# One of three projections of a hybrid decoder step goes from plain products to Strassen's scheme, and a merge pair becomes the last unit of the recurrent stage

## The chip, the cores and the metric

The kernel runs on one core of one Trainium2 chip. The metric is device time in microseconds (us) of one execution; lower is better. The engines are named as the profile names them: PE (matmuls; PEld is its loading of weights), DVE (vector engine), ACT (scalar engine), POOL (GpSimd) and SP, from whose queue nearly all transfers are issued.

## What is computed

One step of a decoder layer for a prompt of 2048 rows and for 8 single-row samples, all in float32, with D = 1024. Cut to what matters here:

```python
h = rmsnorm(x, norm_g) * (1 + scale) + shift
q, k, v, ga, xr, gr, ma, mr = split(h @ w_in)
ya = band_attention(rmsnorm(q), rmsnorm(k), v) * silu(ga)
yr = rglru(causal_conv(xr)) * silu(gr)
merged = sigmoid(ma) * (ya @ w_pa) + sigmoid(mr) * (yr @ w_pr)
y = x + gate * (merged @ w_out)
```

## The kernel before

**Precision and slots.** Every float32 operand of a large product is split into a high and a low part in a shorter format (`split_to`: ACT casts the high part, DVE subtracts it to get the low part). A product is then three matmuls per 128 rows of the contraction: high by high, high by low, low by high. The unit of planning is a slot: 4 row blocks by 3 matmuls = 12 matmuls of 128 x 512 into one PSUM bank.

**Two halves.** The prompt is worked on in two halves of 1024 rows (s = 0, then s = 1; the samples ride along in the second). Each half runs attention and then a line of slots (`stages`), transposed: channels on partitions, positions along the free dimension, 512 at a time. The line of a half is: three units that finish the previous stage, the attention's gate, four pairs for the recurrent branch (`rnn(p)`), pairs for the merge gates (`merge`), then the projection of the attention's branch (`pa`), that of the recurrent branch (`pr`) and the output (`out`).

**Two kinds of unit.** `Plain` makes 128 output channels by 1024 positions in 4 slots: per unit 2 splits of weights, and 2 evacuations of a PSUM bank. `Fast` is Strassen's scheme (in Winograd's form) on a 2 x 2 grid: 256 output channels by 1024 positions in 7 slots, where plain products take 8. It works on sums and differences of the four blocks of weights (`s1` to `s4`, on DVE) and of the activations (T1 to T4); per unit 7 splits of weights, 3 banks that are copied out by ACT, 3 that DVE adds to them, and one that is used from PSUM. `pair(a, b)` alternates the slots of two units. Before the change `w_in`'s columns and the output use `Fast`; `pa` and `pr` use `Plain`.

**What sets the order.** `Line` keeps, for each slot, a list of other work with a rank (evacuations first, then splits of weights, then forms of activations, then the chains of the recurrent branch, then stores and loads). All engines run in their program's order, so this list is the order. A unit's weights are loaded 7 slots ahead of their use and split 2 slots ahead. An unsplit input is loaded 3 slots ahead of its split (`load_split`).

**Around the change.** The recurrent chain of one pair (`chain`, 4 pieces of 512 positions: convolution, split, gates, a scan) begins 12 slots after the pair's first slot and ends some 24 slots after the pair's last one. The order of pairs before is: attention gates 2 and 3; rnn 0; merge 1; rnn 1; merge 2; rnn 2; merge 3; rnn 3; then `pa`. The activations of the input `h` (7 forms by 4 blocks) fill all 28 large tiles of the ring S until the last unit, marked `final`, gives them back. The ring B has 35 tiles of 512 columns for everything else. Tensors in DRAM: `yad` (attention times gate, the input of `pa`), `tmad` and `tmd` (tanh of the merge gates), `t1d` (what `pa` leaves), `sgd`, `yrd`, `mgd`. `phase_h`, in the first half alone, prepares the second half's `h` (loads of `x`, row norms, transposes) beside `pa`.

```python
EVAC, SIDE, SPLIT, FORM, CHAIN, LATE, STORE, LOAD = range(8)
PROD = (("A11", "x11", "X"), ("A12", "x21", "Y"), ("S2", "T2", "X"), ("S1", "T1", "Y"), ("S3", "T3", "X"),
        ("S4", "x22", "Y"), ("A22", "T4", "X"))
AHEAD, LOADS = 2, 7
```

Of the kernel before, what the change touches and what calls it, by code (L numbers as in the profile page):

```python
# [12 lines left out]
F32 = mybir.dt.float32  # L13
# [28 lines left out]
def tile_hybrid_step(ctx: ExitStack, tc: tile.TileContext, x_prompt, x_sample, cache_k, cache_v, state_conv,  # L42
# [191 lines left out]
    V.memset(q1, 0.25)  # L234

# [107 lines left out]
    for t in wgr + [hsF, yaF]:  # L343
# [8 lines left out]
                                     for t in ("yad", "tmad", "tmd", "sgd", "yrd", "t1d", "mgd"))  # L352
    Gd = dp.tile([P, D], F32, tag="Gd", name="Gd")
# [57 lines left out]
    def phase_h(line, t0):  # L411

        def group(g, t0):
            xts = []

            def load(i):
                xts.append(S([D]))
                r0 = 1024 + g * 512 + i * P
                ld.dma_start(xts[i], xp[r0:r0 + P, :])

            def turn(f):
                ps = PT()
                for i in range(4):
                    T_.transpose(ps[:, i * P:(i + 1) * P], xts[i][:, f * P:(f + 1) * P], ident)
                line.after(1, EVAC, lambda: h_evac(1, ps, 512, f, g * 512, None))
                if f == KT - 1:
                    free(*xts)

            for i in range(4):
                line.on(t0 + 2 * i, LOAD, lambda i=i: load(i))  # L430
                line.on(t0 + 4 + 2 * i, CHAIN, lambda i=i: rms_rows([xts[i][:, h * 512:(h + 1) * 512] for h in range(2)], P))
# [669 lines left out]
    class Fast:  # L1101
# [3 lines left out]
        def __init__(self, line, F, src, evac, samples=None, base=None, late=False):  # L1105
            self.line, self.F, self.src, self.evac, self.samples = line, F, src, evac, samples
            self.base, self.late, self.early = base, late, 0
# [27 lines left out]
        def place(self, s):  # L1135
# [6 lines left out]
            for i, j in ((0, 0), (1, 0), (0, 1), (1, 1)) if late else ((0, 0), (1, 0), (1, 1), (0, 1)):  # L1142
                line.on(s[0] - (3 if late and j == 1 else LOADS + self.early), LOAD, lambda i=i, j=j: self.load(i, j))
# [109 lines left out]
    def stages(s, hT, hT1=None, side=None):  # L1253
# [348 lines left out]
        pair(attn_gate(2), attn_gate(3))  # L1602
        for p in range(4):
            end = rnn(p)
            if p < 3:
                pair(merge(OFF_MA, p + 1, tmad, maS), merge(OFF_MR, p + 1, tmd, mrS))
# [23 lines left out]
        yax, yrx = xtiles(), xtiles()  # L1630
        quarters = [(4 * h + k, c) for h in range(2) for c in range(2) for k in range(4)]
        for i, (k, c) in enumerate(quarters):
            load_split(yad, yax, k, c, rnn_end - 11 + 10 * i // 16, 3)

        def load_pair_rows(w, c0):
            wr = w[:, c0:c0 + P].rearrange("(G gg j d) c -> G gg d j c", G=2, gg=2, j=4)

            def load(t, h):
                for gg in range(2):
                    ld.dma_start(t[gg * 64:gg * 64 + 64], wr[h, gg])  # L1640
            return load

        def pa(f):
            tm = {}

            def load(c):
                tm[c] = Tt([512])
                ld.dma_start(tm[c], chunk(tmad, f, c))

            def evac(c, ps):  # L1650
                V.scalar_tensor_tensor(tm[c], tm[c], 1.0, ps, op0=ALU.add, op1=ALU.mult)
                line.after(1, STORE, lambda: store(c))
# [525 lines left out]
```

## Time and profile before

| | before |
|---|---|
| median of 3 runs | 1969.95 us (1969.76 to 1970.19) |
| the profiled execution, its own time | 1970.57 us |
| its span, first to last instruction | 1968.9 us |
| PE busy | 1918.9 us (97%), 11504 matmuls |
| DVE busy | 1376.8 us (70%) |
| ACT busy | 985.0 us (50%) |
| POOL busy | 391.3 us (20%) |
| DMA | 286.61 MB, mean 146 GB/s |

The profiled execution's own time is 1.7 us over its span and 0.6 us over the median. Busy shares are means over the whole execution; a stage is read from a window of its own. Matmuls overlap in the records, so the price of one is read from the starts of two groups and the count between them, not from the mean duration.

### The profile page before, as it was taken

How to read it: one execution, taken by the hardware profiler on the slowest of the kernel's cores; microseconds unless marked ns; L12 is line 12 of the kernel's file. 1: busy time of each engine (PE TensorE's matmuls, PEld its weight loads, DVE VectorE, ACT ScalarE, POOL GpSimd, SP SyncE). 2: the span in 40 equal slices, each digit the busy share in tenths (PEclk: the TensorE clock that was granted, in tenths of full speed). 3: DMA queues.
4: the chain of work that ended last, by engine and by line, in shares of the span. 5: the costliest groups of instructions: out<-in, count | busy, mean ns of one | idle time of the engine just before them, and what ended most of it. 6: DMA issues, size and time to landing. Idle time of an engine off the chain costs nothing. (4 is left out here: it accounts for less than half of the span.)

```text
span 1968.9 us, 32371 instructions
## 1 busy us (share of the span) xinstructions
PE 1918.9 (97%) x11504; PEld 1569.0 (80%) x11504; DVE 1376.8 (70%) x2862; ACT 985.0 (50%) x2167; POOL 391.3 (20%) x476
## 2 busy tenths in 40 slices
PE   6899999999999999999999999999999999999999
PEld 4798986778888878877898888777887887777777
DVE  3557778567887876587735776776677879755965
ACT  4435665336575766323424555543475667532321
POOL 2213443000111113150022333300010201111600
PEclk9899999999999999999999999999999999999999
DMA  9521125652433567976611111544233325458673
GB/s 280 175 65 51 48 77 158 202 171 93 138 118 100 176 190 251 330 243 191 228 47 49 55 34 51 160 124 151 82 119 108 126 93 167 144 170 300 214 236 108
DMA packets 307686, 286.61 MB, mean 146 GB/s; under 512 B 57073, under 2 KB 224229, under 8 KB 307486
## 3 DMA queue, kind: packets, MB, share of 16 engines
q1 hardware_dynamic: 307398, 282.41, 45.8%
q0 software_dynamic: 128, 2.15, 0.3%
q8 instruction: 90, 1.47, 0.3%
q14 instruction: 70, 0.57, 0.1%
HBM read 200.69 MB, written 85.93 MB: 146 GB/s over the span
## 5 line engine op out<-in xcount | busy, mean ns | idle before, releaser
L60 PE MATMUL pg<-S,B 128*128 128x512 f32 (+1 forms) x4224 | 1003.7, 392 | 4.2 <-DVE B L60 3.8
L60 PEld LDWEIGHTS pg<-S,B 128*128 128x128 f32 (+1 forms) x4224 | 773.9, 188 | 188.6 <-issue 11.1
L60 DVE TENSOR_TENSOR B<-B,B 128x512 fp32r<-128x512 f32 (+1 forms) x732 | 540.9, 761 | 145.8 <-ACT B L60 136.0
L60 PE MATMUL pq<-S,B 128*128 128x512 f32 (+2 forms) x1920 | 412.2, 379 | 6.7 <-DVE B L60 6.6
L60 PEld LDWEIGHTS pq<-S,B 128*128 128x128 f32 (+1 forms) x1920 | 317.0, 188 | 85.2 <-DVE B L60 10.6
L60 POOL TENSOR_TENSOR B<-B,B 128x512 f32<-128x512 f32 x128 | 191.4, 1513 | 921.5 <-DVE B L60 363.5
L60 ACT CAST B<-B 128x512 fp32r<-128x512 f32 x468 | 279.9, 617 | 111.4 <-DVE B L60 71.5
L60 PE MATMUL pg<-B,S 128*128 128x256 f32 x1872 | 243.3, 286 | 0.0
L60 PEld LDWEIGHTS pg<-B,S 128*128 128x128 f32 x1872 | 228.1, 189 | 10.1 <-issue 9.4
L60 DVE TENSOR_TENSOR S<-B,S 128x512 fp32r<-128x512 f32 x184 | 144.6, 814 | 25.9 <-ACT S L60 25.7
L60 ACT CAST S<-B 128x512 fp32r<-128x512 f32 x184 | 109.3, 620 | 94.0 <-DVE B L60 40.7
L60 ACT ACTIVATE B<-B 128x512 f32<-128x512 f32 (+1 forms) x150 | 93.1, 629 | 117.0 <-DVE B L60 109.0
L60 ACT ACTIVATE B<-B,M 128x129 f32<-128x129 f32 x260 | 102.6, 396 | 91.3 <-DVE M L60 87.1
L60 DVE SCALAR_TENSOR_TENSOR B<-B,pg 128x512 f32<-128x512 f32 x78 | 53.1, 682 | 72.9 <-PE pg L60 63.1
L60 ACT COPY H<-pt 128x256 f32<-128x256 f32 (+1 forms) x55 | 18.5, 337 | 160.9 <-PE pt L60 160.9
L60 DVE TENSOR_TENSOR B<-pq,B 128x512 f32<-128x512 f32 x96 | 65.9, 686 | 44.3 <-PE pq L60 38.3
L60 POOL TENSOR_TENSOR B<-B,M 128x512 f32<-128x512 f32 x64 | 68.6, 1093 | 122.8 <-DVE M L60 122.8
L60 ACT COPY B<-pg 128x512 f32<-128x512 f32 x80 | 46.8, 586 | 89.4 <-PE pg L60 81.1
L60 ACT ACTIVATE B<-pg 128x512 f32<-128x512 f32 x76 | 45.2, 595 | 85.3 <-PE pg L60 85.3
L60 POOL TENSOR_TENSOR M<-M,mhalf 128x8 f32<-128x8 f32 (+4 forms) x70 | 83.8, 1198 | 5.8
L60 DVE SCALAR_TENSOR_TENSOR B<-B,VT,B 128x512 f32<-128x512 f32 x96 | 81.2, 846 | 2.3
L60 DVE TENSOR_TENSOR B<-pt,mcT 128x512 f32<-128x512 f32 x64 | 41.7, 686 | 47.4 <-ACT B L60 45.5
(201 smaller groups left out, 1718.6 us busy)
## 6 DMA issues: line engine op xcount, KB each, us to landing
B<-in_w_in_dram SPq DMA_DIRECT2D x144, 256.0 KB
B<-in_w_in_dram SPq DMA_DIRECT2D x128, 128.0 KB
B<-yad SPq DMA_DIRECT2D x56, 256.0 KB
B<-hd SPq DMA_DIRECT2D x48, 256.0 KB
B<-in_w_out_dram SPq DMA_DIRECT2D x48, 256.0 KB
S<-in_w_ada_dram SPq DMA_DIRECT2D x32, 256.0 KB
S<-in_x_prompt_dram SPq DMA_DIRECT2D x16, 512.0 KB
hd<-B SPq DMA_DIRECT2D x32, 256.0 KB
```

The lines of the kernel that those rows point to most:

```text
L60: ins = fn(*args, **kw)
```

## The change

The projection `pa` is made of 4 `Fast` units in 2 pairs (28 slots) where 8 `Plain` units (32 slots) stood, in each half. Its evacuation goes to DVE for one block in four; for the other three ACT adds 1 to the merge gate's tanh (`plus`) and POOL multiplies. The four differences of its input are made earlier, by `differences`: 4 times 4 loads from `yad`, 4 subtractions on POOL, 4 stores to the new DRAM tensor `yfd`. The 7 forms by 4 blocks are then loaded and split by `form_y` (28 loads and splits where 16 stood). The pair of attention gates 2 and 3 moves behind rnn 0, and each merge pair moves one place, so that merge 3 is the last pair before `pa`. `phase_h` starts 8 slots later, counted from the recurrent stage's end, and holds its rows in tiles of ring B. Weights of `pa` are loaded 5 slots ahead.

```diff
+    onec = C([P, 1], tag="onec")
+    V.memset(onec, 1.0)
...
+    yfd = dp.tile([2, 4, 4, P, 512], F32, tag="yfd", name="yfd")
...
-                xts.append(S([D]))
+                xts.append([Tt([512]) for _ in range(2)])
                 r0 = 1024 + g * 512 + i * P
-                ld.dma_start(xts[i], xp[r0:r0 + P, :])
+                for h in range(2):
+                    ld.dma_start(xts[i][h], xp[r0:r0 + P, h * 512:(h + 1) * 512])
...
-            self.base, self.late, self.early = base, late, 0
+            self.base, self.late, self.early, self.ahead = base, late, 0, LOADS
...
-                line.on(s[0] - (3 if late and j == 1 else LOADS + self.early), LOAD, lambda i=i, j=j: self.load(i, j))
+                line.on(s[0] - (3 if late and j == 1 else self.ahead + self.early), LOAD, lambda i=i, j=j: self.load(i, j))
...
-        pair(attn_gate(2), attn_gate(3))
         for p in range(4):
             end = rnn(p)
-            if p < 3:
-                pair(merge(OFF_MA, p + 1, tmad, maS), merge(OFF_MR, p + 1, tmd, mrS))
+            if p == 0:
+                pair(attn_gate(2), attn_gate(3))
+                ga_end = len(seq)
+            else:
+                pair(merge(OFF_MA, p, tmad, maS), merge(OFF_MR, p, tmd, mrS))
         seq[-1][0].final = True
         rnn_end = len(seq)
 
...
-        for i, (k, c) in enumerate(quarters):
-            load_split(yad, yax, k, c, rnn_end - 11 + 10 * i // 16, 3)
...
+
+        FY = {n: [None] * 4 for _, n, _ in PROD}
+
+        def differences(k, t):
+            x = {}
+
+            def load():
+                for n, f, c in (("x11", k, 0), ("x12", k, 1), ("x22", k + 4, 1), ("x21", k + 4, 0)):
+                    x[n] = Tt([512])
+                    ld.dma_start(x[n], chunk(yad, f, c))
+
+            def sub(a, b, o, n):
+                G_.tensor_tensor(x[o], x[a], x[b], op=ALU.subtract)
+                line.after(2, STORE, lambda: st.dma_start(yfd[s, n, k], x[o]))
+
+            def first():
+                sub("x12", "x11", "x11", 0)
+                sub("x22", "x12", "x12", 2)
+
+            def second():
+                x["T2"] = Tt([512])
+                sub("x22", "x11", "T2", 1)
+                sub("x21", "T2", "x21", 3)
+
+            line.on(t, LOAD, load)
+            line.on(t + 4, FORM, first)
+            line.on(t + 6, FORM, second)
+            line.on(t + 9, EVAC, lambda: free(*x.values()))
+
+        for k in range(4):
+            differences(k, ga_end + (6, 11, 27, 32)[k])
+
+        def form_y(n, k, t):
+            src = {"x11": (k, 0), "x21": (k + 4, 0), "x22": (k + 4, 1)}.get(n)
+            box = []
+
+            def load():
+                box.append(Tt([512]))
+                ld.dma_start(box[0], chunk(yad, *src) if src else yfd[s, int(n[1]) - 1, k])
+
+            def split():
+                FY[n][k] = S([2, 512], F32R)
+                split_to(FY[n][k][:, 0, :], FY[n][k][:, 1, :], box[0])
+                free(box[0])
+
+            line.on(t - 3, LOAD, load)
+            line.on(t, FORM, split)
+
+        for i, (n, k) in enumerate([(n, k) for _, n, _ in PROD for k in range(4)]):
+            form_y(n, k, rnn_end - 9 + 18 * i // 25)
+
+        def pa(p):
+            tm = {}
+
+            def load_w(t, i, j):
+                wr = w_proj_attn[0][:, (2 * p + i) * P:(2 * p + i + 1) * P].rearrange(
+                    "(G gg j d) c -> G gg d j c", G=2, gg=2, j=4)
                 for gg in range(2):
-                    ld.dma_start(t[gg * 64:gg * 64 + 64], wr[h, gg])
-            return load
-
-        def pa(f):
-            tm = {}
-
-            def load(c):
-                tm[c] = Tt([512])
-                ld.dma_start(tm[c], chunk(tmad, f, c))
-
-            def evac(c, ps):
-                V.scalar_tensor_tensor(tm[c], tm[c], 1.0, ps, op0=ALU.add, op1=ALU.mult)
-                line.after(1, STORE, lambda: store(c))
-
-            def store(c):
-                st.dma_start(chunk(t1d, f, c), tm[c])
-                free(tm[c])
-
-            z, d = zS[:, f:f + 1, :], maS[:, f:f + 1, :]
-            u = Plain(line, yax, load_pair_rows(w_proj_attn[0], f * P), evac,
-                      sample(yaF, z, lambda: V.scalar_tensor_tensor(d, d, 1.0, z, op0=ALU.add, op1=ALU.mult)))
-            t0 = len(seq)
-            seq.extend((u, n) for n in range(4))
-            for c in range(2):
-                line.on(t0 + c, LOAD, lambda c=c: load(c))
-            return u
-
-        for f in range(KT):
-            u = pa(f)
-        u.gone = set(u.order)
+                    ld.dma_start(t[gg * 64:gg * 64 + 64], wr[j, gg])
+
+            def load(i, j):
+                tm[i, j] = Tt([512])
+                ld.dma_start(tm[i, j], chunk(tmad, 2 * p + i, j))
+
+            def plus(i, j):
+                A.activation(tm[i, j], tm[i, j], AF.Identity, bias=onec)
+
+            def evac(i, j, x, t):
+                y = tm[i, j]
+                if t is None:
+                    V.scalar_tensor_tensor(y, y, 1.0, x, op0=ALU.add, op1=ALU.mult)
+                else:
+                    G_.tensor_tensor(y, y, x, op=ALU.mult)
+                    free(t)
+                line.after(1 if t is None else 2, STORE, lambda: store(i, j))
+
+            def store(i, j):
+                st.dma_start(chunk(t1d, 2 * p + i, j), tm[i, j])
+                free(tm[i, j])
+
+            z, d = zS[:, 2 * p:2 * p + 2, :], maS[:, 2 * p:2 * p + 2, :]
+            u = Fast(line, FY, load_w, evac,
+                     sample(yaF, z, lambda: V.scalar_tensor_tensor(d, d, 1.0, z, op0=ALU.add, op1=ALU.mult)))
+
+            def loads(t0):
+                for n, i, j in ((1, 0, 0), (4, 1, 1), (5, 0, 1), (6, 1, 0)):
+                    line.on(t0 + 2 * n - 4, LOAD, lambda i=i, j=j: load(i, j))
+                    if n < 6:
+                        line.on(t0 + 2 * n, LATE, lambda i=i, j=j: plus(i, j))
+
+            return u, loads
+
+        for p in range(0, 4, 2):
+            (a, la), (b, lb) = pa(p), pa(p + 1)
+            a.ahead = b.ahead = 5
+            t0 = pair(a, b)
+            la(t0)
+            lb(t0 + 1)
+        b.final = True
         pa_end = len(seq)
         for i, (k, c) in enumerate(quarters):
-            load_split(yrd, yrx, k, c, pa_end - 8 + i // 2 if i < 8 else pa_end - 3 + (i - 8) // 2, 3)
+            load_split(yrd, yrx, k, c, pa_end - 10 + 3 * i // 4, 3)
 
         def pr(f):
             ts = {}
...
+            phase_h(line, rnn_end + 12)
             for k in range(KT):
...
-            line.steps(sample_attn(), range(7, 30), SIDE)
+            line.steps(sample_attn(), list(range(7, 27)) + [38], SIDE)
```

Three places in the engines' order. On DVE where the projection starts: below, before the change, are the 11 rows from the last recurrent pair's two last slots into the projection's first units. B is ring B, S ring S (an S row is a split of an activation), pg and pq are PSUM, VT holds the convolution's weights.

```order
L60 TENSOR_TENSOR B_7819<-B_7691,B_7818 128x512
L60 SCALAR_TENSOR_TENSOR B_7816<-B_7816,pg_7419 128x512
L60 SCALAR_TENSOR_TENSOR B_7847<-B_7548,VT_105,B_7847 128x512 x3
L60 TENSOR_TENSOR B_7874<-B_7743,B_7873 128x512
L60 TENSOR_TENSOR B_7882<-B_7847,B_7881 128x512
L60 SCALAR_TENSOR_TENSOR B_7824<-B_7824,pg_7803 128x512
L60 SCALAR_TENSOR_TENSOR B_7879<-B_7879,B_7767 128x512
L60 SCALAR_TENSOR_TENSOR B_7856<-B_7856,pg_7826 128x512
L60 TENSOR_TENSOR B_7929<-B_7800,B_7928 128x512
L60 SCALAR_TENSOR_TENSOR B_7877<-B_7932,B_7877 128x512
L60 TENSOR_TENSOR B_7976<-B_7858,B_7975 128x512
```

The same place after the change, 12 rows of the projection's first two slots:

```order
L60 TENSOR_TENSOR B_7829<-B_7826,B_7829 128x512
L60 TENSOR_TENSOR B_7826<-B_7974,B_7826 128x512
L60 TENSOR_TENSOR B_8020<-B_7835,B_8019 128x512
L60 TENSOR_TENSOR B_8023<-B_7869,B_7872 128x512
L60 TENSOR_TENSOR S_8025<-B_7916,S_8025 128x512
L60 TENSOR_TENSOR B_7869<-B_7866,B_7869 128x512
L60 TENSOR_TENSOR B_7866<-B_8023,B_7866 128x512
L60 TENSOR_TENSOR B_8054<-B_7875,B_8053 128x512
L60 TENSOR_TENSOR S_8057<-B_7954,S_8057 128x512
L60 TENSOR_TENSOR S_8060<-B_7956,S_8060 128x512
L60 SCALAR_TENSOR_TENSOR B_7944<-B_8028,B_7944 128x512
L60 TENSOR_TENSOR B_8087<-B_7826,B_8086 128x512
```

Before, a unit's evacuations (those that read pg), a split of weights and the chain's work alternate; now forms of weights, splits of weights, splits of activations and the chain's work stand behind each other. The evacuations of these slots are ACT's or come later.

On DVE at the end of the first recurrent pair's chain, between the two scans (rows that read HC; the order prints a scan as a SCALAR_TENSOR_TENSOR). Before, beside merge 1:

```order
L60 SCALAR_TENSOR_TENSOR B_5620<-B_5590,HC_124,B_5565 128x512
L60 COPY HC_124<-B_5620 128x1
L60 SCALAR_TENSOR_TENSOR B_5814<-B_5326,VT_105,B_5814 128x512 x3
L60 TENSOR_TENSOR B_5661<-pq_5672,B_5661 128x512
L60 TENSOR_TENSOR B_5835<-B_5694,B_5834 128x512
L60 SCALAR_TENSOR_TENSOR B_5692<-B_5668,HC_124,B_5645 128x512
L60 COPY HC_124<-B_5692 128x1
L60 TENSOR_TENSOR B_5846<-B_5814,B_5845 128x512
L60 TENSOR_TENSOR B_5865<-B_5696,B_5698 128x512
```

After, beside attention gates 2 and 3:

```order
L60 SCALAR_TENSOR_TENSOR B_5299<-B_5265,HC_126,B_5237 128x512
L60 COPY HC_126<-B_5299 128x1
L60 SCALAR_TENSOR_TENSOR B_5507<-B_4931,VT_107,B_5507 128x512 x3
L60 TENSOR_TENSOR B_5464<-B_5464,B_5465 128x512
L60 TENSOR_TENSOR B_5342<-pq_5354,B_5342 128x512
L60 SCALAR_TENSOR_TENSOR B_5488<-B_5488,B_5315 128x512
L60 TENSOR_TENSOR B_5533<-B_5376,B_5532 128x512
L60 SCALAR_TENSOR_TENSOR B_5374<-B_5349,HC_126,B_5325 128x512
L60 COPY HC_126<-B_5374 128x1
L60 TENSOR_TENSOR B_5544<-B_5507,B_5543 128x512
L60 TENSOR_TENSOR B_5488<-B_5488,B_5489 128x512
```

Between the scans there are now one multiplication by the attention (B_5465) and one SiLU step more, and another product (B_5489) behind the second.

On POOL in the second recurrent pair and its merge pair. Before:

```order
L60 TENSOR_TENSOR B_5620<-B_5620,B_5726 128x512
L60 TENSOR_TENSOR B_5692<-B_5692,B_5764 128x512
L60 DMA out_dram<-in_cache_v_dram 8x2x16256
L60 TENSOR_TENSOR B_5843<-B_5843,B_5841 128x512
L60 TENSOR_TENSOR B_5938<-B_5938,B_5936 128x512
L60 TENSOR_TENSOR B_5909<-B_5909,B_6005 128x512
L60 TENSOR_TENSOR B_5982<-B_5982,B_6028 128x512
L60 DMA out_dram<-in_state_conv_dram 8x2048
L60 TENSOR_TENSOR B_6317<-B_6317,B_6315 128x512
```

After; the products of the chain (four in a group, as before) are followed by the differences:

```order
L60 TENSOR_TENSOR B_5615<-B_5615,B_5715 128x512
L60 TENSOR_TENSOR B_5692<-B_5692,B_5738 128x512
L60 TENSOR_TENSOR B_5766<-B_5768,B_5766 128x512
L60 TENSOR_TENSOR B_5768<-B_5770,B_5768 128x512
L60 TENSOR_TENSOR B_5921<-B_5770,B_5766 128x512
L60 TENSOR_TENSOR B_5772<-B_5772,B_5921 128x512
L60 DMA out_dram<-in_cache_v_dram 8x2x16256
L60 TENSOR_TENSOR B_5895<-B_5897,B_5895 128x512
L60 TENSOR_TENSOR B_5897<-B_5899,B_5897 128x512
L60 TENSOR_TENSOR B_6079<-B_5899,B_5895 128x512
L60 TENSOR_TENSOR B_5901<-B_5901,B_6079 128x512
```

Each `differences` adds four subtractions, in two pieces that are two slots apart; four such groups are added in each half.

## Rows read from the trace of the kernel before

**Rows 1.** The page: busy time of each engine, share of the span, instructions.

```profile
PE 1918.9 (97%) x11504; PEld 1569.0 (80%) x11504; DVE 1376.8 (70%) x2862; ACT 985.0 (50%) x2167; POOL 391.3 (20%) x476
```

**Rows 2.** Busy by window: projection of the attention's branch, first and second half.

```profile
core 0: us, PE busy (x) PEld busy (x) DVE busy (x) ACT busy (x) POOL busy (x), PEclk, DMA share, GB/s
706.10:805.90 99.80, 99.66 (x456) 81.10 (x455) 64.77 (x100) 61.67 (x111) 20.72 (x32) 1.00 0.81 257
1679.00:1781.80 102.80, 102.80 (x555) 80.53 (x555) 61.90 (x113) 47.70 (x86) 12.33 (x8) 1.00 0.59 180
```

**Rows 3.** Timeline of PE, groups of matmuls: start, duration, count, idle before.

```profile
652.50 5.73 PE L60 MATMUL pq<-S,B 128*128 128x512 f32 x24
...
698.09 2.61 PE L60 MATMUL pq<-S,B 128*128 128x512 f32 x10 [0.45 <-DVE B L60]
...
722.80 19.55 PE L60 MATMUL pg<-S,B 128*128 128x512 f32 x84
742.19 1.54 PE L60 MATMUL pt<-B,H 128*128 128x512 f32 x6
...
882.09 22.10 PE L60 MATMUL pg<-S,B 128*128 128x512 f32 x94 [1.00 <-DVE B L60]
```

**Rows 4.** The same view, the wait at the projection's start in the second half.

```profile
1670.32 2.60 PE L60 MATMUL pq<-S,B 128*128 128x512 f32 x10 [1.60 <-DVE B L60]
```

**Rows 5.** Groups of DVE instructions by form, 640 to 900 us: count, busy, mean ns.

```profile
L60 DVE TENSOR_TENSOR S<-B,S 128x512 fp32r<-128x512 f32 x56 | 46.4, 859 | 3.0 <-ACT S L60 2.9
L60 DVE SCALAR_TENSOR_TENSOR B<-B,pg 128x512 f32<-128x512 f32 x33 | 22.4, 681 | 26.5 <-PE pg L60 26.5
```

**Rows 6.** Timeline of DVE, single groups with and without POOL beside them.

```profile
649.53 2.32 DVE L60 SCALAR_TENSOR_TENSOR B<-B,VT,B 128x512 f32<-128x512 f32 x3
...
653.40 2.39 DVE L60 TENSOR_TENSOR B<-B,B 128x512 fp32r<-128x512 f32 x2
...
658.21 1.28 DVE L60 TENSOR_TENSOR_SCAN B<-B,HC,B 128x512 f32<-128x512 f32 x1
...
659.59 3.23 DVE L60 SCALAR_TENSOR_TENSOR B<-B,VT,B 128x512 f32<-128x512 f32 x3
...
692.29 2.39 DVE L60 TENSOR_TENSOR S<-B,S 128x512 fp32r<-128x512 f32 x2
...
697.96 1.28 DVE L60 TENSOR_TENSOR S<-B,S 128x512 fp32r<-128x512 f32 x2
```

**Rows 7.** Timeline of POOL at the same times.

```profile
659.91 1.58 POOL L60 TENSOR_TENSOR B<-B,B 128x512 f32<-128x512 f32 x1 [5.27 <-DVE HC L60]
...
691.89 1.64 POOL L60 TENSOR_TENSOR B<-B,B 128x512 f32<-128x512 f32 x1 [5.08 <-DVE HC L60]
```

**Rows 8.** Busy by window: around the scans of the second and third recurrent pair, and late in the second half.

```profile
565.00:592.00 27.00, 27.00 (x119) 21.91 (x118) 26.68 (x37) 21.45 (x36) 6.03 (x4) 1.00 0.36 125
649.00:681.00 32.00, 32.00 (x139) 25.92 (x138) 31.68 (x47) 24.97 (x42) 6.02 (x4) 1.00 0.52 170
...
1641.00:1672.00 31.00, 29.40 (x128) 23.49 (x127) 28.19 (x56) 20.77 (x37) 5.48 (x4) 1.00 0.50 162
```

**Rows 9.** Groups of ACT instructions by form, whole execution.

```profile
L60 ACT CAST B<-B 128x512 fp32r<-128x512 f32 x468 | 279.9, 617 | 111.4 <-DVE B L60 71.5 <-DMA B<-in_w_proj_rnn_dram 17.7 <-DMA B<-mgd 12.4
```

**Rows 10.** The chain that ended last, pieces ahead of the wait at 1670.32.

```profile
1662.01 2.56 DMA B<-yad
1664.56 2.37 DVE S L60 x2
...
1668.83 1.44 DVE B L60
```

**Rows 11.** Busy by window, the first half's second projection.

```profile
800.00:850.00 50.00, 50.00 (x229) 40.62 (x228) 25.64 (x34) 15.00 (x25) 9.49 (x7) 1.00 0.94 320
```

**Rows 12.** Waits of SP's queue, longest in total: us, times, longest.

```profile
SPq L60 <- DVE B L60: 405.1, 169, 17.8
```

More of the change, by code (lines that the diff above doesn't have):

```diff
@@ L423, in turn @@
                 for i in range(4):
-                    T_.transpose(ps[:, i * P:(i + 1) * P], xts[i][:, f * P:(f + 1) * P], ident)
+                    T_.transpose(ps[:, i * P:(i + 1) * P], xts[i][f // 4][:, f % 4 * P:(f % 4 + 1) * P], ident)
                 line.after(1, EVAC, lambda: h_evac(1, ps, 512, f, g * 512, None))
-                if f == KT - 1:
-                    free(*xts)
+                if f % 4 == 3:
+                    free(*(x[f // 4] for x in xts))
             for i in range(4):
                 line.on(t0 + 2 * i, LOAD, lambda i=i: load(i))
-                line.on(t0 + 4 + 2 * i, CHAIN, lambda i=i: rms_rows([xts[i][:, h * 512:(h + 1) * 512] for h in range(2)], P))
+                line.on(t0 + 4 + 2 * i, CHAIN, lambda i=i: rms_rows(xts[i], P))
             for f in range(KT):
@@ L1628, in xtiles @@
             return [[None, None] for _ in range(KT)]
-        yax, yrx = xtiles(), xtiles()
+        yrx = xtiles()
         quarters = [(4 * h + k, c) for h in range(2) for c in range(2) for k in range(4)]
-        for i, (k, c) in enumerate(quarters):
-            load_split(yad, yax, k, c, rnn_end - 11 + 10 * i // 16, 3)
-        def load_pair_rows(w, c0):
-            wr = w[:, c0:c0 + P].rearrange("(G gg j d) c -> G gg d j c", G=2, gg=2, j=4)
-            def load(t, h):
-                for gg in range(2):
-                    ld.dma_start(t[gg * 64:gg * 64 + 64], wr[h, gg])
-            return load
@@ L1707, in pr @@
             return u
+        u = None
         for f in range(KT):
@@ L1836, in stages @@
                 line.on(t, LOAD, lambda dst=dst, src=src: G_.dma_start(dst, src))
-            phase_h(line, rnn_end + 4)
+            phase_h(line, rnn_end + 12)
             for k in range(KT):
```

## The prediction

> **What bounds the kernel now.** First the page's busy shares [rows 1]: PE works 97% of the span, DVE 70%. These are means over unlike stages, so next the window of the projection that is rewritten [rows 2]: PE 99.66 of 99.8 us in the first half and all of 102.8 in the second, DVE some 65% and 60%. In this stage only fewer matmuls can save time. Last PE's own waits: 0.45 us before 698.09 and 1.60 us before 1670.32, both for DVE and both just ahead of the projection [rows 3, 4]. The reader should see that PE waits where DVE is full, and that DVE is full around the scans of each recurrent pair: 26.68 of 27.0 us and 31.68 of 32.0 us [rows 8]. PE does not wait there before the change, but little is in hand. The two splits at 653.40 end at 655.79, so the first is done by 655.2; PE's group of 24 from 652.50 [rows 3] has its second slot at 652.50 + 12 x 0.231 = 655.27, and reads the low part of that slot's weights in its third matmul, at 655.73 [rows 6]. That is a lead of 0.5 us, less than one DVE instruction.
>
> **What PE saves.** Four units of 7 slots replace eight of 4 in each half: 28 slots for 32. At 12 matmuls a slot, two halves lose 96 matmuls. The group of 84 that starts at 722.80 is followed by the next at 742.19 [rows 3]: 19.39 / 84 = 0.231 us each, in a window with the granted clock at 1.00 [rows 2]. 96 x 0.231 = **22.2 us**. The two waits of 2.05 us at the old start belong to an order that is gone, and I count them as gone; what comes in their place is priced below.
>
> **What DVE gets, first place.** Attention gates 2 and 3 now run beside the scans of the first recurrent pair, where a merge pair ran. Each of their evacuations adds a SiLU step and a product, and six fall in the six slots around the scans: 12 instructions. DVE's pitch is 0.60 us for one of 512 columns: two in 1.28 us at 697.96 [rows 6], where 0.68 is one alone with its tail. 12 x 0.60 = 7.2 us. The like windows of the later pairs have 0.32 us idle [rows 8], so nearly all of it is lateness. Against it stand the leads: 0.5 us at the tightest slot, more at its neighbours, because a split stands two slots ahead in the program. Bounds: 7.2 - 0.3 - 0.5 = 6.4 us if the tightest slot decides, 2 us if most is taken up in the slots with more lead. I take 4.5 us. In the second half the samples' work lengthens PE's slots there, as DVE's lower share late in that half shows, 28.19 of 31.0 us [rows 8]: 0 to 4 us, I take 1.5.
>
> **What DVE gets, second place.** The projection's input used to be 16 splits and its weights 16. Now there are 28 of each, and 16 sums of weights and 12 additions of PSUM banks come in; 12 of the 16 evacuations by DVE leave. Over the whole stage DVE still has room. The crowding is where it starts: in the 18 slots from the last three of the last merge pair on, I count by the order of the engines about 64 single DVE instructions, a convolution of three (2.32 us at 649.53) and four scans with their copies (1.28 + 0.15) [rows 6]: 64 x 0.60 + 2.32 + 5.7 = 46.4 us. PE needs 18 x 2.77 = 49.9 us there, and 52.7 with two groups of transposes of 1.4 [rows 3]. So far it fits.
>
> But 13 POOL products lie in the same slots. Where POOL runs a product, DVE's work on two SBUF operands stretches: three convolution steps take 3.23 us in place of 2.32 (+0.91) beside POOL's 1.58 at 659.91, two splits 2.39 in place of 1.28 (+1.11) beside its 1.64 at 691.89 [rows 6, 7]. DVE's steps that read PSUM keep to a mean of 681 ns beside a mean of 859 for the splits [rows 5]. Taking 0.95 a product, 13 x 0.95 = 12.4 us, and DVE needs 58.8 us against PE's 52.7: 6.1 us late. Less about 1 us of lead, that is **5 us** of waits in the first half; bounds 0 (the leads and PE's waits elsewhere take it) and 9 (the scans' queue starts late as well). In the second half PE has the samples' columns and no transposes to hide, and only the tail of the crowding is left: 3 us, bounds 0 and 7.
>
> [...]
>
> **What else moves.** ACT gets 24 more casts, 24 sums and 24 copies; in those 18 slots 67 instructions of 0.617 [rows 9] are 41 us of 52.7, hidden behind PE, and late copies would hold PSUM banks if that cover went. The differences are 16 subtractions a half on POOL, 20% busy [rows 1], beside merge and recurrent pairs; each costs DVE up to 1.1 us, at most four together near the scans: 0 to 3 us, I take 0, since most pieces stand between the scans' windows. Their 16 loads and 16 stores, and 12 more loads of forms, move 44 x 0.262 = 11.5 MB a half, where DMA's share is 0.36 to 0.52 [rows 8]. The second half's preparation moves 8 slots later, next to a stretch with a share of 0.94 [rows 11] and a wait of 1.00 us before 882.09 [rows 3]: 0 to 3 us, I take 0, since PE waits nowhere inside the second projection today. The constant `onec`, the moved step of the samples and weights loaded 5 slots ahead cost nothing: 5 slots are 13.9 us against a load's 2.56 [rows 10].
>
> **The sum.** 1970.57 (the profiled execution; span 1968.9) - 22.2 - 2.05 + 4.5 + 1.5 + 5 + 3 = 1960.3. That execution lies 0.6 us above the median, so 1959.7 as a median; the lower bounds weigh a little more than the upper ones, because each wait that PE takes gives DVE time for the next: **1959 us**.
>
> **The rivals.** (a) The forecast: DVE late at the two places, 9 to 19 us of new waits, 1954 to 1965. Chance 0.60.
> (b) The lateness is absorbed. For it: DVE has 35% free over the stage, splits are emitted two slots early, and PE reads forms one after the other. Against it: the full windows and the 0.5 us lead. Then 1970.6 - 24.2 - 0.6 = 1945.8, up to 1953 with a few waits left. Chance 0.20.
> (c) Each POOL product holds DVE for its whole 1.6 us. For it: the stretches of about 1 us; against it: those same rows, in which 0.5 us per product is left over. 13 x 0.6 = 8 us more in the first half, and up to 4 in the second if its PE slack is used up: 1965 to 1971. Chance 0.14.
> (d) The other side: the forms' loads arrive late. SP's queue waits long for tiles to come free, 405 us over 169 times [rows 12], and the ring B is fuller now. One load of `yad` (2.56 us from issue to landing, then a split of 2.37 and DVE work of 1.44 [rows 10]) was part of the wait of 1.60 at 1670.32 [rows 4]. Each half has seven groups of four forms; if PE waited for each of the 14 groups, what decides is 24.2 / 14 = 1.7 us a group, and at a whole landing of 2.56 it would be 36 us, so 1970 - 24 + 36 = 1982. Against it: loads are issued three slots, 8.3 us, ahead. Chance 0.06.
>
> **How the numbers follow.** A change of 0.2% is 3.9 us, about what this measurement can tell: faster means below 1966.0, slower above 1973.9. Faster holds (a), (b) and an eighth of (c)'s weight or a little more: 0.84. The rest of (c) and a sliver of (d) are no change: 0.11. Slower is most of (d): 0.05. The range leaves out the lowest of (b), the highest of (c) and (d): 1948 to 1968. The likeliest case alone runs from 1954 to 1965.
>
> **What would show it.** Right: 11408 matmuls on the page, 96 fewer than in [rows 1]; PE's waits named as for DVE at the end of the first pair's chain and in the projection's first 15 slots, each of 0.3 to 2 us, none in its second half; DVE full in both places; the stretched convolution and split rows beside POOL's products. Wrong: waits named for a DMA from `yad` or `yfd` (then (d)); PE's busy share over 98% with no new waits (then (b)); waits at PSUM banks that ACT holds, or waits in the second projection at the DMA's 0.94, which I price at nothing.

## The result: slower by 0.4%

The changed kernel takes 1977.4 us (median; 1974.62 to 1980.13) beside 1969.59 us for the kernel before in the same comparison: a ratio of 1.0040, interval 1.0028 to 1.0051. The forecast was 1959, with 0.05 for slower. The profiled execution has 1977.35 us and a span of 1975.6, 6.7 us more than before. The busy line of the page, beside [rows 1]:

```profile
PE 1904.1 (96%) x11408; PEld 1551.5 (79%) x11408; DVE 1473.8 (75%) x2939; ACT 1034.8 (52%) x2259; POOL 486.8 (25%) x532
```

PE lost its 96 matmuls. Its busy time fell by 14.8 us where 22.2 were worked out, and its idle time rose from 50.0 to 71.5 us. DVE rose by 97 us for only 77 more instructions. What PE waited for, in groups (us, times, longest):

```profile
PE pg L60 <- DVE B L60: 16.6, 13, 2.4
PE pq L60 <- DVE B L60: 10.0, 15, 1.3
...
PE pt L60 <- DVE CO L60: 3.8, 1, 3.8
...
PE pt L60 <- DVE xrS L60: 1.3, 1, 1.3
```

Before, the last two were not there, and the first two were these:

```profile
PE pq L60 <- DVE B L60: 6.6, 8, 1.6
...
PE pg L60 <- DVE B L60: 3.8, 4, 1.2
```

That makes 16.2 + 5.1 of the 21.5 us of idle time. Where they lie is read from PE's timeline (start, duration, count, idle before):

```profile
461.74 4.14 PE L60 MATMUL pg<-S,B 128*128 128x512 f32 x10 [1.88 <-DVE B L60]
...
469.12 3.02 PE L60 MATMUL pg<-S,B 128*128 128x512 f32 x12 [1.85 <-DVE B L60]
...
516.83 2.58 PE L60 MATMUL pq<-S,B 128*128 128x512 f32 x10 [0.77 <-DVE B L60]
...
560.58 2.59 PE L60 MATMUL pq<-S,B 128*128 128x512 f32 x10 [0.37 <-DVE B L60]
...
584.54 2.59 PE L60 MATMUL pq<-S,B 128*128 128x512 f32 x10 [1.28 <-DVE B L60]
...
721.67 2.59 PE L60 MATMUL pg<-S,B 128*128 128x512 f32 x10 [1.65 <-DVE B L60]
...
724.86 1.42 PE L60 MATMUL pt<-B,H 128*128 128x512 f32 x5 [0.36 <-DVE B L60]
...
727.16 2.59 PE L60 MATMUL pg<-S,B 128*128 128x512 f32 x10 [0.41 <-DVE B L60]
...
745.17 2.57 PE L60 MATMUL pq<-S,B 128*128 128x512 f32 x10 [0.38 <-DVE B L60]
...
757.40 2.60 PE L60 MATMUL pq<-S,B 128*128 128x512 f32 x10 [0.71 <-DVE B L60]
759.84 0.63 PE L60 MATMUL pg<-S,B 128*128 128x512 f32 x2
761.99 11.06 PE L60 MATMUL pg<-S,B 128*128 128x512 f32 x46 [1.52 <-DVE B L60]
...
884.21 3.04 PE L60 MATMUL pg<-S,B 128*128 128x512 f32 x12 [0.47 <-DVE B L60]
889.29 22.02 PE L60 MATMUL pg<-S,B 128*128 128x512 f32 x94 [2.03 <-DVE B L60]
...
1424.79 4.54 PE L60 MATMUL pg<-S,B 128*128 128x512 f32 x12 [2.44 <-DVE B L60]
...
1537.68 3.05 PE L60 MATMUL pg<-S,B 128*128 128x512 f32 x12 [0.81 <-DVE B L60]
1541.38 2.59 PE L60 MATMUL pg<-S,B 128*128 128x512 f32 x10 [0.65 <-DVE B L60]
...
1683.60 2.60 PE L60 MATMUL pq<-S,B 128*128 128x512 f32 x10 [0.44 <-DVE B L60]
...
1705.41 0.41 PE L60 MATMUL pt<-ident,H 128*128 128x128 f32 x2 [1.33 <-DVE xrS L60]
...
1732.46 2.59 PE L60 MATMUL pq<-S,B 128*128 128x512 f32 x10 [1.02 <-DVE B L60]
1738.88 0.66 PE L60 MATMUL pt<-ident,CO 128*96 128x128 f32 x2 [3.83 <-DVE CO L60]
```

The reader should see five kinds of place: the moved attention gates (near 460 and 1425), the differences (516 to 585 and near 1540), the projection's start (721 to 762, and 1683 and 1732 in the second half), the end of the second projection (884 and 889), and two groups of transposes for the samples and the state in the second half (1705 and 1738). The duration of ten matmuls at 461.74 is 4.14 us where 2.6 is usual. Windows show why (columns as in [rows 2]):

```profile
459.00:462.00 3.00, 1.12 (x5) 0.64 (x4) 3.00 (x6) 2.04 (x4) 0.00 (x0) 1.00 0.36 123
462.00:465.50 3.50, 3.50 (x10) 2.69 (x10) 3.47 (x5) 2.31 (x5) 2.20 (x2) 0.51 0.36 122
...
1424.60:1428.00 3.40, 3.21 (x8) 2.53 (x9) 3.37 (x7) 0.89 (x2) 0.00 (x0) 0.51 0.27 103
...
1738.60:1742.10 3.50, 3.22 (x9) 2.61 (x10) 3.34 (x9) 0.00 (x0) 1.28 (x1) 0.51 0.78 214
```

Behind three of the longer waits the granted clock is 0.51 in these windows, for some 3.4 us. The matmuls there take about 1.5 us longer by the rows: 4.14 us for 2.6, and 4.54 for the 3.0 of twelve. Last, the window of the projection itself, beside [rows 2], and the crowded one beside [rows 11]:

```profile
719.40:808.50 89.10, 83.93 (x364) 65.34 (x362) 83.89 (x114) 63.26 (x117) 33.48 (x29) 1.00 0.83 279
1696.30:1788.80 92.50, 86.17 (x436) 67.74 (x434) 80.33 (x125) 57.90 (x108) 28.40 (x17) 0.98 0.74 236
...
800.00:850.00 50.00, 50.00 (x242) 40.83 (x241) 28.72 (x41) 23.59 (x45) 13.14 (x19) 1.00 1.01 348
```

The windows of the projection are shorter, 89.1 us for 99.8 and 92.5 for 102.8, but that is not its gain, since they hold different other work. Before, 384 of the 456 and 555 matmuls recorded in them are the projection's (32 slots), after, 336 of 364 and 436: transposes of the second half's preparation and small products lie elsewhere now. Of the new waits about half lie ahead of the projection and half inside it. In the part of the second projection shown, DMA is at 1.01 and PE has no idle time; its two waits come later, at 884 and 889.

### The profile page after: what moved, and what is told of

The parts are those of the page before. It is cut to its first block, busy times and chain, and to the rows that moved or that the text cites. A ratio compares the mean times of both kernels' runs of the same rounds, so it can differ in the third digit from the quotient of the medians.

```text
span 1975.6 us, 32787 instructions
## 1 busy us (share of the span) xinstructions
PE 1904.1 (96%) x11408; PEld 1551.5 (79%) x11408; DVE 1473.8 (75%) x2939; ACT 1034.8 (52%) x2259; POOL 486.8 (25%) x532
## 5 line engine op out<-in xcount | busy, mean ns | idle before, releaser
L60 PE MATMUL pg<-S,B 128*128 128x512 f32 (+1 forms) x3840 | 920.3, 393 | 17.0 <-DVE B L60 16.6
L60 PEld LDWEIGHTS pg<-S,B 128*128 128x128 f32 (+1 forms) x3840 | 704.6, 189 | 188.8 <-DVE B L60 22.4
L60 DVE TENSOR_TENSOR B<-B,B 128x512 fp32r<-128x512 f32 (+1 forms) x788 | 602.8, 788 | 122.3 <-ACT B L60 107.0
L60 POOL TENSOR_TENSOR B<-B,B 128x512 f32<-128x512 f32 x184 | 287.7, 1580 | 857.0 <-ACT B L60 376.5
L60 PE MATMUL pq<-S,B 128*128 128x512 f32 (+2 forms) x2208 | 483.6, 382 | 10.3 <-DVE B L60 10.0
L60 PEld LDWEIGHTS pq<-S,B 128*128 128x128 f32 (+1 forms) x2208 | 369.9, 188 | 104.1 <-DVE B L60 18.3
L60 ACT CAST B<-B 128x512 fp32r<-128x512 f32 x492 | 295.0, 618 | 130.4 <-DVE B L60 89.4
L60 DVE TENSOR_TENSOR S<-B,S 128x512 fp32r<-128x512 f32 x208 | 184.3, 910 | 24.2 <-ACT S L60 24.2
L60 ACT CAST S<-B 128x512 fp32r<-128x512 f32 x208 | 123.6, 621 | 71.0 <-DVE B L60 30.9
L60 POOL TENSOR_SCALAR M<-M 128x8 f32<-128x8 f32 (+5 forms) x71 | 15.3, 215 | 273.6 <-DVE M L60 268.8
```

What stands on the lines that cost most here:

```text
L60: ins = fn(*args, **kw)
```

## The experiments

Ratios are to the kernel before, run beside each group; that of the changed kernel is 1.0040.

**1. The differences' subtractions on DVE.** Theory 1: a POOL product of two SBUF operands takes more from DVE than the step would take there.

```diff
-                G_.tensor_tensor(x[o], x[a], x[b], op=ALU.subtract)
+                V.tensor_tensor(x[o], x[a], x[b], op=ALU.subtract)
```

> The changed kernel with one edit: the 16 subtractions of the differences of each half run on DVE instead of POOL. Theory 1 (a POOL product of two SBUF operands takes about 0.9 us from DVE, more than the 0.60 us that DVE needs for it itself; the waits of PE at the start of merge 1, slots 73 to 76 and 89 to 97 of the first half, come from that): DVE's busy time falls by about 32 x 0.3 = 10 us, those waits (3.6 us in the first half, about 3 in the second) shrink by half or more, and the time falls by 2 to 5 us against the changed kernel, to 1972 to 1975. Rival (what is late is DVE by its own instructions, and POOL's work beside it is as good as free): DVE gets 32 x 0.60 = 19 us more, the waits grow, and the time rises by 3 to 8 us, to 1980 to 1985.

Ratio 1.0010 (0.9998 to 1.0023), 1974.16 us: theory 1, with 0.30% or 5.9 us, a little over its 2 to 5. DVE executes 32 more instructions and is busy for less:

```profile
PE 1902.4 (96%) x11408; PEld 1552.6 (79%) x11408; DVE 1467.7 (74%) x2971; ACT 1034.9 (52%) x2259; POOL 437.6 (22%) x500
```

6.1 us less, where 10 were expected, with 32 steps of 0.68 recorded more: each of the subtractions had taken (6.1 + 21.8) / 32 = 0.87 us from DVE, or 0.79 if a step counts with its pitch of 0.60. One place shows it. In the changed kernel, POOL's row and then DVE's beside it:

```profile
512.64 2.99 POOL L60 TENSOR_TENSOR B<-B,B 128x512 f32<-128x512 f32 x2 [8.81 <-PE pt L60]
```

```profile
512.68 4.09 DVE L60 TENSOR_TENSOR B<-B,B 128x512 f32<-128x512 f32 x3
```

In the experiment DVE does its three steps and both subtractions in less time:

```profile
512.23 3.35 DVE L60 TENSOR_TENSOR B<-B,B 128x512 f32<-128x512 f32 x5
```

The waits of 0.77, 0.37 and 1.28 us from 516 to 585 leave 0.44; those of the second half (0.81, 0.65, 0.26 and 0.24 near 1540) leave 0.95. In run 5, which has the new order and no differences, there is no wait at these places.

**2. All evacuations of the projection on DVE.**

```diff
-                if t is None:
-                    V.scalar_tensor_tensor(y, y, 1.0, x, op0=ALU.add, op1=ALU.mult)
-                else:
-                    G_.tensor_tensor(y, y, x, op=ALU.mult)
+                V.scalar_tensor_tensor(y, y, 1.0, x, op0=ALU.add, op1=ALU.mult)
...
-                    if n < 6:
-                        line.on(t0 + 2 * n, LATE, lambda i=i, j=j: plus(i, j))
```

> The changed kernel with one edit: the projection's three other evacuations per unit are done by DVE too, in one step (tanh + 1) x product; the 24 sums on ACT and 24 products on POOL are gone. Theory 1 (0.9 us of DVE per POOL product against 0.60 for the step on DVE): DVE falls by about 24 x 0.3 = 7 us, PE's waits inside the projection of the first half (5.0 us recorded, from 719 to 762) fall by 1 to 2 us, the time by 1 to 3 us, to 1974 to 1976. Rival (POOL's work is free): 24 x 0.60 = 14 us more on DVE, the waits grow, and the time rises by 2 to 6 us, to 1979 to 1983.

1.0027 (1.0014 to 1.0039), 1976.88 us. DVE's busy time falls by 6.6 us with 24 more steps, as theory 1 says, but the ratio can't be told from the changed kernel's. PE's waits of 0.71 and 1.52 near 760 became one of 2.08, and those of the projection's first half fell from 5.0 to 4.5 us in all.

**3. The transposes of the state three slots later.**

```diff
-            line.steps(state_out(), [end + 1], SIDE)
+            line.steps(state_out(), [end + 4], SIDE)
```

> The changed kernel with one edit: PE's two transposes of the recurrent state in the second half stand 3 slots later. Theory 2 (PE waits 3.83 us before 1738.88 only because DVE, late in the projection, has not yet copied the state, and the clock is granted at half for the 3.41 us behind that wait): the wait and the lower clock go, the time falls by 3.8 + 1.7 = 5.5 us, less what DVE's lateness takes back at the next split, so 4 to 5.5, to 1972 to 1973.5. Rival (DVE is behind there anyway, and the wait only moves to the next split of weights): 0 to 1.5 us.

1.0023 (1.0012 to 1.0034), 1975.36 us. The wait of 3.83 is gone, and the twelve matmuls next to the old place take 3.05 us for 4.35; a split of weights then makes PE wait where it did not before:

```profile
1735.79 2.57 PE L60 MATMUL pg<-S,B 128*128 128x512 f32 x10 [1.54 <-DVE B L60]
```

3.83 + 1.5 - 1.54 = 3.8 us by the trace, 3.3 by the ratios, whose intervals overlap: just under theory 2's range. Most of that wait was the transposes' own, a part DVE's lateness.

**4. The old order of pairs, with Strassen's projection.** `pair(attn_gate(2), attn_gate(3))` stands ahead of the loop again, and the second half's preparation at `rnn_end + 16`.

> Strassen's scheme kept, the order of pairs undone: the pair of attention gates 2 and 3 stands before the first recurrent pair again and the recurrent pair is the last before the projection; the differences keep their place relative to the pairs, and the second half's preparation starts 4 slots later still, which the ring of tiles needs. Theory 3 (the first place of the change costs about 10 us: waits of 1.88 + 1.85 + 2.44 us and twice 1.7 us of lower clock, and some smaller ones): these go; but the last recurrent pair's chain, with four scans, now lies beside the projection's forms, so that the waits at its start grow by 5 to 20 us: 1972 to 1988. Rival (the order is not what costs): within 2 us of the changed kernel, 1975.5 to 1979.5, with the same waits at the same instructions of the projection.

1.0084 (1.0067 to 1.0100), 1988.35 us. The waits near 460 and 1425 are gone, and the projection's start loses more, for example:

```profile
792.84 4.08 PE L60 MATMUL pg<-S,B 128*128 128x512 f32 x10 [2.49 <-DVE B L60]
...
816.73 0.48 PE L60 MATMUL pt<-ident,B 128*128 128x128 f32 x1 [3.14 <-DVE B L60]
```

So the new order is the better one for this projection, though it has a price.

**5. The new order alone,** with the plain projection of before (and the samples' last attention step moved with it).

```diff
-        pair(attn_gate(2), attn_gate(3))
         for p in range(4):
             end = rnn(p)
-            if p < 3:
-                pair(merge(OFF_MA, p + 1, tmad, maS), merge(OFF_MR, p + 1, tmd, mrS))
+            if p == 0:
+                pair(attn_gate(2), attn_gate(3))
+            else:
+                pair(merge(OFF_MA, p, tmad, maS), merge(OFF_MR, p, tmd, mrS))
```

> The kernel before with the new order of pairs alone (attention gates 2 and 3 behind the first recurrent pair, merge 3 last; the samples' last attention step moves with it); plain projection, no differences. Theory 3 (the gates beside the scans cost about 10 us: 6.2 us of waits and two stretches of half clock, 3.4 us): 6 to 9 us over the kernel before, that is 1975.5 to 1979, with a wait near 460 us of the span and one near 1425, and without the waits of 0.45 and 1.60 at the projection's start. Rival (the order is free, and the differences and the forms of the projection are the whole loss): 2 us under to 1 us over the kernel before.

1.0049 (1.0034 to 1.0064), 1980.25 us: 9.7 us for the order, just past the upper end of theory 3's range. The two places of the gates are there, and one at the projection's start that theory 3 did not have:

```profile
461.36 4.15 PE L60 MATMUL pg<-S,B 128*128 128x512 f32 x10 [1.81 <-DVE B L60]
468.73 3.01 PE L60 MATMUL pg<-S,B 128*128 128x512 f32 x12 [1.83 <-DVE B L60]
...
718.75 2.60 PE L60 MATMUL pg<-S,B 128*128 128x512 f32 x10 [2.46 <-DVE B L60]
...
1424.28 4.50 PE L60 MATMUL pg<-S,B 128*128 128x512 f32 x12 [2.46 <-DVE B L60]
```

On this order Strassen's projection gained 1.0049 - 1.0040, about 2 us of its 22, and the difference lies within the two intervals.

**6. The edits of 1, 2 and 3 together.**

> The changed kernel with three edits together: subtractions of the differences on DVE, all evacuations of the projection on DVE, transposes of the state 3 slots later. If the three costs are separate, their ratios add: -0.3, -0.13 and -0.17%, so about 0.998 of the kernel before, 3 to 5 us under it. Rival (they all draw on one lateness of DVE at the projection's start): no better than the best single edit, 1.000 to 1.001 of the kernel before.

0.9998 (0.9987 to 1.0010), 1970.91 us: level with the kernel before and nearer to the rival. Added up, the three ratios would give 0.998; what is missing, 0.18%, is less than an interval is wide, so whether edits 2 and 3, which touch one stretch, share a lateness stays open.

**7. The recurrent chain's products on DVE too.**

```diff
-                    G_.tensor_tensor(v["i"], v["i"], v["r"], op=ALU.mult)
+                    V.tensor_tensor(v["i"], v["i"], v["r"], op=ALU.mult)
...
-                    G_.tensor_tensor(v["s"], v["s"], v["g"], op=ALU.mult)
+                    V.tensor_tensor(v["s"], v["s"], v["g"], op=ALU.mult)
```

> As the three edits, and the recurrent chain's 64 POOL products too run on DVE. Theory 1 (0.9 us of DVE per POOL product against 0.60 for its own): DVE busy falls by 64 x 0.3 = 19 us against the three edits, the wait near 460 us and that near 1425 (1.9 + 1.9 and 2.4 us in the changed kernel) fall by 1 to 2 us each and with them a stretch of half clock: 3 to 6 us less than the three edits. Rival (the chain's products are spread where DVE is idle, and its own 64 steps now stand in front of the splits): 0 to 6 us more.

0.9954 (0.9939 to 0.9969), 1960.23 us: faster than both kernels, and by more than theory 1 asked for. Against run 6 (DVE 1463.2 us) DVE does 64 more steps in 17.1 us less, 0.95 us a product (0.87 with the pitch of 0.60):

```profile
PE 1896.8 (97%) x11408; PEld 1549.6 (79%) x11408; DVE 1446.1 (74%) x3059; ACT 1021.6 (52%) x2235; POOL 300.9 (15%) x412
```

The span is 11.0 us shorter than run 6's: 3.1 us of it PE's idle time, 7.9 its busy time, which the number of matmuls does not explain. The mean granted clock goes with it, 0.996 beside 0.992, but not all of that is the edit's: PE's group of 48 matmuls that starts at 364.96 in run 6 starts at 361.39 here, 3.6 us earlier, and up to there the two programs are the same. By the ratios the edit gives 0.44%, 8.7 us. It frees DVE's time and it also shortens a product for the chain that waits for it, from some 1.6 us on POOL to 0.7 on DVE; these runs do not tell the two apart. Two waits of the first place are left:

```profile
458.80 2.58 PE L60 MATMUL pg<-S,B 128*128 128x512 f32 x10 [0.99 <-DVE B L60]
...
466.29 4.53 PE L60 MATMUL pg<-S,B 128*128 128x512 f32 x12 [3.47 <-DVE B L60]
```

**8. The gates' SiLU step and product behind the splits of their slot,** on top of run 7: the rank of `silu` and `mult` is LATE, and the attention's tile is fetched at the slot's end.

> As the run before it (all on DVE), and the SiLU step and the product of attention gates 2 and 3 stand behind the splits of weights in their slot (as before in the same slot, only later in it; the attention's tile is fetched at the slot's end). Theory 3 (PE waits because these 12 steps stand ahead of the splits that it needs): the waits near 460 and 1425 us shrink by 2 to 5 us together, and the lower clock behind them goes: 3 to 6 us less than the run before it. Rival (DVE is short in total there, and the order inside a slot only moves the lateness to the chain): 0 to 1 us.

1.0008 (0.9998 to 1.0019), 1972.10 us: both expectations missed, some 11 us over run 7. The profiled execution, 1967.49 us, is 7.3 us over run 7's, 5.0 of it PE's idle time. The edit also moved the fetch and the product of an attention gate ahead of the recurrent stage, and there DVE now waits for the late tile itself, and PE for DVE:

```profile
349.97 0.69 DVE L60 TENSOR_TENSOR B<-B,B 128x512 f32<-128x512 f32 x1 [5.50 <-DMA B<-yad]
```

```profile
352.05 5.39 PE L60 MATMUL pg<-S,B 128*128 128x512 f32 x22 [3.15 <-DVE B L60]
```

Run 7 has neither wait, so this run is no clean test of theory 3: a good part of its loss is the late fetch. At the places that were meant, the wait near 1423 is 2.28 for 1.55 us, and the second one near 466 grew though the splits now came first:

```profile
471.48 5.46 PE L60 MATMUL pg<-S,B 128*128 128x512 f32 x12 [4.32 <-DVE B L60]
```

That points at another cause for it, theory 4. In the changed kernel DVE's step that ends just before PE goes on at 469.12 is the SiLU step that reads its input from PSUM:

```profile
468.30 0.67 DVE L60 SCALAR_TENSOR_TENSOR B<-B,pg 128x512 f32<-128x512 f32 x1
```

One block in four of a gate stays in its PSUM bank until that step, so a late DVE holds the bank that PE needs next.

**9. The kernel before with the chain's products on DVE,** the edit of run 7 alone.

> The kernel before with one edit: the recurrent chain's 64 POOL products run on DVE. Theory 1 (0.9 us of DVE per POOL product against 0.60): DVE busy falls by some 19 us or more, PE's waits of 0.45 and 1.60 us at the projection's start shrink, and the time falls by 1 to 4 us, since little of PE's time is lost there. Rival (the 10 us that the same edit gave on top of the three edits are a gain that any version of this kernel would have, so the Strassen projection is worth nothing): 8 to 11 us under the kernel before.

0.9978 (0.9969 to 0.9987), 1966.44 us: 4.3 us, just past theory 1's range and far from the rival's. PE's waits at the projection's old start (0.45 and 1.60) are gone. DVE falls by 13.2 us, where 19 or more were expected: (13.2 + 43.5) / 64 = 0.89 us a product, or 0.81 with the pitch. Between this and run 7 the order and Strassen's projection, with the edits of runs 1 to 3, are worth 0.24%, 4.7 us; the two intervals just touch.

**10. Run 7, and ACT copies that bank out.**

```diff
             def evac(i, j, x, t):
+                if t is None and p > 1:
+                    t = Tt([512])
+                    A.copy(t, x)
+                    x = t
```

> As the run with everything on DVE (1960 us), and the last block of each attention gate 2 and 3 is copied out of its PSUM bank by ACT, so that its SiLU step on DVE no longer holds the bank. Theory 4 (the second wait near 466 us, 3.47, and the one near 1415, 1.55, are for a PSUM bank that DVE's late SiLU step frees): both waits shrink to under 1 us in sum and the half clock behind the first goes, 3 to 6 us less, 1954 to 1957. Rival (DVE is late for the splits as well, and the wait comes back at the next of them): 0 to 1.5 us less.

0.9951 (0.9936 to 0.9966), 1960.48 us. The 3.47 us are gone, so the wait was for the bank, and the time stays, as the rival says: the splits of the next slots are late in its place, 2.5 us in three waits.

```profile
460.32 2.60 PE L60 MATMUL pg<-S,B 128*128 128x512 f32 x10 [0.99 <-DVE B L60]
465.32 2.59 PE L60 MATMUL pg<-S,B 128*128 128x512 f32 x10 [0.53 <-DVE B L60]
469.65 3.05 PE L60 MATMUL pq<-S,B 128*128 128x512 f32 x12 [1.28 <-DVE B L60]
473.39 2.60 PE L60 MATMUL pq<-S,B 128*128 128x512 f32 x10 [0.68 <-DVE B L60]
```

**11. The same edit on the changed kernel alone.**

> The changed kernel with that edit alone: ACT copies the last block of attention gates 2 and 3 out of its bank. Theory 4: of the waits near 460 us the first (1.88, a split of weights) stays, the second (1.85) goes, the 2.44 near 1425 goes and with it a stretch of half clock: 4 to 6 us less than the changed kernel, 1971 to 1973. Rival: the waits come back at the next splits, 0 to 1.5 us less.

1.0025 (1.0016 to 1.0034), 1976.34 us, about 3 us by the ratios, between the two, though the intervals overlap. The 1.85 became 0.41 and 0.67, the 2.44 near 1425 became 0.38, 0.88 and 0.45.

**12. Run 7 with the old order of pairs** (and the preparation at `rnn_end + 16`).

> As the run with everything on DVE (1960 us), with the old order of pairs (attention gates 2 and 3 first, a recurrent pair last). Theory 3 (Strassen's projection can't stand beside the last recurrent pair's scans): the first place's waits and clock (about 8 us) go, but the projection's start loses more: 1963 to 1975. Rival (with POOL's products gone the projection's start has room, and the moved gates are all that is left of the loss): 1950 to 1957.

0.9985 (0.9976 to 0.9994), 1968.05 us: theory 3. The waits are at the projection's start again, 3.09 and 2.37 the longest, and 3.5 us in all for DMA of the projection's weights (1.0 in run 7).

## Why the prediction was wrong

The saving was right: 96 matmuls fewer on the page. The two large terms of DVE's lateness held as sums. **First place:** 4.5 + 1.5 forecast, 1.88 + 1.85 + 2.44 = 6.2 us of waits measured; the mechanism was half right, since two of the three waits were for a PSUM bank that the SiLU step holds, not for a split (runs 10 and 11). **Second place:** 5 us forecast in the first half, 5.0 measured (the rows from 721 to 762); 3 in the second half, 0.44 + 1.02 = 1.5 measured. The 2.05 us of the old waits did go. That the 5 us fit so well is in part luck: with POOL's products there on DVE (run 7) 3.0 of the 5.0 us of waits remain, where the prediction's own count without the stretch, 46.4 + 13 x 0.60 = 54.2 us against 52.7 with 1 us of lead, would leave about 0.5.

What failed are the things taken at nothing, and together they exceed the forecast gain:

- **The half clock behind waits.** The sum counts idle time alone. Behind the waits of 2.44 and 3.83 us, at a granted clock of 0.51, it costs some 1.5 us each (twelve matmuls take 4.54 us behind the one and 4.35 behind the other), 3.1 together. Behind the wait of 1.88 it costs nothing of its own: from that restart to the next it is 7.38 us (461.74 to 469.12), and 7.38 us too in runs 1 and 2, where the ten matmuls behind the first wait take 2.6 us, those behind the second are the slow ones (5.46 us for twelve) and the second wait is longer instead (3.42 and 3.41 us). In run 1:

```profile
460.18 2.59 PE L60 MATMUL pg<-S,B 128*128 128x512 f32 x10 [1.87 <-DVE B L60]
...
467.56 5.46 PE L60 MATMUL pg<-S,B 128*128 128x512 f32 x12 [3.42 <-DVE B L60]
```

  So DVE sets both restarts, and its lateness in the first half's first place is 1.88 + 1.85 + 1.55 = 5.3 us, the last for the ten slow matmuls (4.14 for 2.59); with 2.44 in the second half, 7.7 for the 6 forecast. The windows above have 0.51 behind the waits of 1.88, 2.44 and 3.83 us; behind the one of 1.85 us it is 1.00 (465.50 to 472.00).
- **The samples' transposes**, 1.33 + 3.83 = 5.2 us. The prediction costed "the moved step of the samples" at nothing and did not look at who waits for DVE besides the splits. The state's copies stand in DVE's queue behind all that makes DVE late, and PE's transposes one slot behind them; run 3 took 3.3 us of it back. The move of that step is not the cause: run 5 has it too and neither wait.
- **The differences**, "I take 0": 2.4 us in the first half and 2.0 in the second, 4.4 together, over the stated bound of 3. The price per product was about right, 0.79 to 0.95 us by runs 1, 7 and 9 against 0.95. The error was to apply it only at the projection's start. That "most pieces stand between the scans' windows" was not checked against the leads there.
- **The end of the second projection**, 0.47 + 2.03 = 2.5 us in the first half against 1.00 before; priced at nothing. The reason given, "PE waits nowhere inside the second projection today", misread its own row: the wait before 882.09 [rows 3] lies inside it, since of the 94 matmuls behind it only the last 24 are the output's. What makes DVE late there was not tested.

3.1 + 5.2 + 4.4 + 1.5 = 14.2 us, and 0.2 that the first two places came out over the sum (7.7 + 5.0 + 1.5 for 14): 1959.7 + 14.4 = 1974.1. The rest to 1977.4 is 3.3 us. A cost that the sum also left out is large enough for it: a wait costs more than its recorded idle time. Between the starts at 757.40 and 761.99 lie 12 matmuls and a wait of 1.52 us, and 4.59 = 12 x 0.231 + 1.52 + 0.30. PE has 30 waits for DVE in the groups above where it had 12; 18 x 0.3 is some 5 us, an estimate from these rows alone. This is also where part of the missing busy time went, 14.8 us saved for 22.2.

One count of the prediction is off without consequence: the "24 more casts" are those of one half, so that ACT executes 92 instructions more.

Of the rivals, (b) and (d) are out: waits came, and none of PE's is for `yad` or `yfd`. Rival (c), a product holding DVE for its whole length, is answered in size: 0.79 to 0.95 us of DVE for products recorded at 1.58 and 1.64 us [rows 7]. What the prediction did not draw from its own number is that 0.95 is more than the 0.60 that the step takes on DVE. Runs 1, 7 and 9 move such products to DVE, and its busy time falls by 6.1, 17.1 and 13.2 us.

Which part lost is told by runs 4, 5, 9, 7 and 12. The order costs 9.7 us by itself, yet Strassen's projection in the old order costs 16.6; in both, most of PE's new waits are for DVE. Once POOL's products stop taking DVE's time, the new order (0.9954) is better than the old (0.9985), and the new order with Strassen's projection is worth some 5 us of the 22 (runs 9 and 7). The rest still goes into waits for DVE; which of DVE's steps could leave it was not tried beyond runs 10 and 11.

## What to carry to other kernels

When PE is full and DVE nearly so, a saving on PE is worth only what DVE can follow: add DVE's new work slot by slot wherever it lands, not only where the changed stage begins, and list everyone who waits for DVE: splits, PSUM banks, small transposes. Before giving a step to POOL to spare DVE, compare what it takes from DVE there (0.8 to 0.95 us here) with what it takes on DVE (0.6). A wait on PE may cost a stretch of half clock on top, as behind waits of 2.44 and 3.83 us here (0.51 for some 3.4 us, 1.5 us lost each), and a removed wait may come back at the next late step. An edit that reorders work can also move a transfer: run 8 was meant to test an order and measured a late fetch.

## What was not expected of the hardware

The same wait is not always followed by slower matmuls. That of 2.44 us at 1424.79 in the changed kernel is followed by a clock of 0.51, and its twelve matmuls take 4.54 us; in run 5 it is 2.46 us and the twelve take 4.50; in runs 1, 2 and 3 it is as long (2.43 to 2.44 us) and the twelve take 3.02 to 3.05 us. Executions of one kernel also spread, and the clock they were granted with them: the kernel before ran, beside runs 5 to 8, from 1966.35 us at a mean of 0.998 to 1977.9 us at 0.992, a spread wider than the change itself, so that effects under about 3 us stay open here.
